# The four weight sums of a seven-product block scheme: written by VectorE instead of GpSimd

## The chip, the cores and the metric

The kernel runs on one core of one Trainium2 chip. The metric is the device time of one execution in microseconds. The engines are TensorE (PE in the profile; PEld is its weight load), VectorE (DVE, `V` in the code), ScalarE (ACT, `S`), GpSimd (POOL, `G`) and SyncE (SP), which issues the DMAs. Each engine works through its own queue in order.

## The reference, cut to what matters

One layer of a diffusion transformer: 2048 latent tokens and 128 prompt tokens of width 1024, differential attention and a short convolution, then a dense feed-forward of hidden width 2816. The change lies in the first half of the feed-forward, the products with `w_ffn_in`:

```python
D_FF = -(-8 * D_MODEL // (3 * 256)) * 256
...
    u = rms_norm(x, g_ffn_pre) * (1.0 + scale_f) + shift_f
    gu = u @ w_ffn_in
    h = jax.nn.silu(gu[..., :D_FF]) * gu[..., D_FF:]
    return x + gate_f * rms_norm(h @ w_ffn_out, g_ffn_post)
```

## The kernel before

The kernel has three long stages: projections and attention, then the feed-forward up products (`gu` and `h`, called the up stage here), then the feed-forward down products (`h @ w_ffn_out`). All numbers are fp32. TensorE multiplies a rounded form (fp32r), so every operand is split in two: `split` makes the rounded high part with a copy on ScalarE (line 81, `CAST` in the trace) and the remainder with a subtraction (line 82), by default on VectorE. Each product is then three matmuls: high by high, high by low and low by high.

The up stage does not multiply the blocks directly. The tokens of a chunk are taken in two halves, and the weights of one block of 128 hidden columns as a 2 by 2 arrangement `a11, a12, a21, a22` (gate and up columns by the two halves of the 1024 inputs), each 128x512. Seven products of combined blocks replace eight. The combinations of the weights are four sums or differences, made by `total` (lines 914 to 917) inside `wi_ops`: `s1 = a21 + a22`, `s2 = s1 - a11`, `s3 = a11 - a21`, `s4 = a12 - s2`. Their buffer `st` has two slots. The seven operands `a11, s1, s2, a12, s3, s4, a22` are split into tiles called `wi`: six of them in three buffers that hold two operands each, the seventh in another pair of buffers. A buffer can be written again when TensorE has done the products that read it.

There are three chunks of tokens (320, 384 and 384 columns wide) and 22 blocks of hidden columns, so 66 units; `wi_ops` runs again for each of them, since the weights are loaded anew for each chunk. A unit has 84 matmuls (7 products, 4 slices of the contraction, 3 matmuls each, lines 954 to 956) into four accumulators `ba` to `bd`. Between products ScalarE copies accumulators (lines 965, 968, 970), VectorE adds (lines 976 `c22` and 979 `u2`, shown as `c` and `u`), and ScalarE, GpSimd (line 982) and VectorE (line 985) form the hidden rows `hid`, which SP stores.

Raw weights come in 512 KB loads, `raw<-in_w_fi`, two for each unit, into the pool `t4` with four slots, one unit ahead. During the first and the second chunk `build_spilled` also prepares the token operands of the following chunk, three times in each: it loads rows into the same `t4` slots (`row`), scales them on GpSimd (line 833), transposes them on TensorE and forms differences on GpSimd (line 857, `td`). Each result is split into `hl`, which has one buffer, and stored to memory (`u2d<-hl`) before the following one may be written. The third chunk has no such work.

The order of the instructions on each engine is not that of the source. A planner orders them when the kernel is compiled, by a simulated run with a table of costs, so it can interleave neighbouring units. Each engine then follows that order and waits where an operand is not ready.

Of the kernel before, what the change touches and what calls it, by code (L numbers as in the profile page):

```python
# [40 lines left out]
def layer(ctx, tc, x_prompt, x_sample, cache_k, cache_v, cond, w_ada, b_ada, gcol,  # L41
# [3 lines left out]
    V, S, G, T = nc.vector, nc.scalar, nc.gpsimd, nc.tensor  # L45
# [33 lines left out]
    def split(h, l, src, eng=None):  # L79

        S.copy(h, src)  # L81
        (eng or V).tensor_tensor(l, src, h.bitcast(F32), op=ALU.subtract)  # L82
# [828 lines left out]
    def wi_ops(raws):  # L911
        a11, a12, a21, a22 = (r[:, i * 512:(i + 1) * 512] for r in raws for i in range(2))

        def total(x, y, op):
            t = sm_.tile([P, 512], F32, tag="st", name="st", bufs=2)
            G.tensor_tensor(t, x, y, op=op)  # L916
            return t

        dst = []
        for k in range(4):  # L920
            if k < 3:
                km = pk.tile([P, NALL], F32R, tag="km", name="wi", bufs=3)
                dst += [(km[:, 1024 * q:1024 * q + 512], km[:, 1024 * q + 512:1024 * q + 1024]) for q in range(2)]
            else:
                q = pk.tile([P, 2, 512], F32R, tag="qt", name="wi", bufs=2)
                dst.append((q[:, 0], q[:, 1]))
        split(*dst[0], a11)
        s1 = total(a21, a22, ALU.add)
        split(*dst[1], s1)
        s2 = total(s1, a11, ALU.subtract)  # L930
        split(*dst[2], s2)
        split(*dst[3], a12)
        s3 = total(a11, a21, ALU.subtract)
        split(*dst[4], s3)
        s4 = total(a12, s2, ALU.subtract)
        split(*dst[5], s4)
        split(*dst[6], a22)
        return dst
# [218 lines left out]
```

## Time and profile before

| what | value |
|---|---|
| time, median of 3 runs | 3038.56 us (3036.72 to 3039.07) |
| profiled execution, time | 3041.68 us |
| profiled execution, span on the core | 3039.9 us |
| TensorE clock granted, mean | 0.987 |
| up stage in the trace | 1520 to 2512 us |

The profile describes one execution, whose own time is 3041.68 us. Engine shares are averages over the three stages. The up stage has three stretches in the trace, one for each chunk: about 1520 to 1840, 1840 to 2190 and 2190 to 2512 us. In a row `wi<-st` names the tile that is written and the tile that is read, `x264` is a count, and `<-` in a wait points to what was waited for.

### The profile page before, as it was taken

To read this page: it belongs to the slowest core of one execution; us is meant where nothing else is said; L and a number is where in the kernel's file an instruction comes from. 1 tells how busy PE (TensorE), PEld (TensorE's weight loads), DVE (VectorE), ACT (ScalarE), POOL (GpSimd) and SP (SyncE) were. 2 spreads that over 40 slices of the span, in tenths; PEclk is the share of its full clock that TensorE was granted. 3 is DMA by queue.
4 is the path that set the end of the run, shared out by engine and by line. 5 is a ranking of instruction groups with operands and counts; after the bars stand their busy time and mean duration, and the time that the engine had idled before them with its cause. 6 is when DMAs were issued, how large, how long until landed. Compare 5 with 4: busy or idle time off the path is not lost.

```text
span 3039.9 us, 47168 instructions
## 1 busy us (share of the span) xinstructions
PE 2902.1 (95%) x16925; PEld 2647.5 (87%) x16925; DVE 1961.1 (65%) x3768; ACT 1466.6 (48%) x2707; POOL 1204.6 (40%) x1106
## 2 busy tenths in 40 slices
PE   6999989999999999999999999999999999999998
PEld 4777789998999998988889989999999998788886
DVE  5998477877888888753367765566555554554443
ACT  5333346665556655554455554445444443434332
POOL 5332135455455454522255654555444440111110
PEclk9999999999999999999999999999999999999999
DMA  8886654454354454457554565445633335766663
GB/s 320 286 306 232 197 177 134 133 168 137 119 178 125 120 165 117 127 182 220 173 159 146 151 196 197 152 152 178 231 102 100 104 103 199 243 218 221 217 218 119
DMA packets 353483, 533.64 MB, mean 176 GB/s; under 512 B 33344, under 2 KB 264928, under 8 KB 351456
## 3 DMA queue, kind: packets, MB, share of 16 engines
q1 hardware_dynamic: 353248, 530.62, 54.2%
q8 instruction: 133, 2.18, 0.3%
q14 instruction: 102, 0.84, 0.1%
HBM read 402.18 MB, written 128.34 MB: 175 GB/s over the span
## 4 chain that ended last, share of the span: by engine, by line
PE 63%; DVE 12%; DMA 10%; issue 8%; POOL 4%; ACT 3%; SPq 0%; DVEq 0%; POOLq 0%; ACTq 0%
PE s L499 7%; PE psg L956 6%; PE psg L954 6%; PE psg L955 6%; PE psy L1086 5%; PE psy L1085 5%; PE psy L1084 5%; PE t L543 3%; DMA u2d<-hl 3%; DVE jv L137 2%; DVE wi L82 2%; PE psx L722 2%; PE psx L723 2%; PE psx L721 2%; PE o L536 2%
## 5 line engine op out<-in xcount | busy, mean ns | idle before, releaser
L954 PE MATMUL psg<-u,wi 128*128 128x384 f32 (+1 forms) x1848 | 607.2, 332 | 26.0 <-ACT wi L81 10.3
L956 PE MATMUL psg<-u,wi 128*128 128x384 f32 (+1 forms) x1848 | 597.1, 329 | 10.0 <-DVE wi L82 10.0
L955 PE MATMUL psg<-u,wi 128*128 128x384 f32 (+1 forms) x1848 | 606.5, 328 | 0.0
L502 DVE TENSOR_SCALAR_CACHE_REDUCE e<-s 128x436 f32<-128x436 f32 (+2 forms) x648 | 373.8, 600 | 85.6 <-PE s L499 68.4
L954 PEld LDWEIGHTS psg<-u,wi 128*128 128x128 f32 x1848 | 349.3, 189 | 36.9 <-ACT wi L81 14.2
L956 PEld LDWEIGHTS psg<-u,wi 128*128 128x128 f32 x1848 | 347.8, 189 | 14.0 <-DVE wi L82 13.7
L499 PE MATMUL s<-km,qt 128*128 128x436 f32 (+1 forms) x1280 | 345.7, 374 | 12.3 <-DVE e L502 8.3
L955 PEld LDWEIGHTS psg<-u,wi 128*128 128x128 f32 x1848 | 350.1, 189 | 0.3
L82 DVE TENSOR_TENSOR wi<-st,wi 128x512 fp32r<-128x512 f32 x264 | 245.2, 932 | 157.7 <-ACT wi L81 154.8
L82 DVE TENSOR_TENSOR wo<-rawo,wo 128x1024 fp32r<-128x1024 f32 x132 | 167.0, 1265 | 252.8 <-ACT wo L81 252.8
L507 ACT ACTIVATE e<-e,nm 128x2176 f32<-128x2176 f32 (+1 forms) x136 | 274.0, 2014 | 78.5 <-DVE nm L506 77.8
L81 ACT CAST wi<-st 128x512 fp32r<-128x512 f32 x264 | 163.2, 619 | 279.2 <-PE psg L956 191.1
L1086 PE MATMUL psy<-wo,hhl 128*128 128x512 f32 x748 | 286.1, 391 | 1.8 <-DVE hhl L82 1.8
L1085 PE MATMUL psy<-wo,hhl 128*128 128x512 f32 x748 | 286.7, 391 | 0.9 <-DVE wo L82 0.9
L1084 PE MATMUL psy<-wo,hhl 128*128 128x512 f32 x748 | 286.3, 391 | 0.0
L81 ACT CAST wo<-rawo 128x1024 fp32r<-128x1024 f32 x132 | 139.1, 1054 | 295.4 <-PE psy L1086 285.2
L82 DVE TENSOR_TENSOR wi<-raw,wi 128x512 fp32r<-128x512 f32 x198 | 233.2, 1194 | 35.6 <-ACT wi L81 29.3
L499 PEld LDWEIGHTS s<-km,qt 128*128 128x128 f32 x1280 | 210.6, 192 | 23.3 <-DVE e L502 14.1
L81 ACT CAST ath<-t 128x512 fp32r<-128x512 f32 (+2 forms) x292 | 157.4, 554 | 114.8 <-PE t L543 112.2
L82 DVE TENSOR_TENSOR atl<-t,ath 128x512 fp32r<-128x512 f32 (+2 forms) x292 | 187.2, 649 | 36.4 <-ACT ath L81 35.6
L1057 POOL TENSOR_TENSOR rr<-rr,mhalf 128x1 f32<-128x1 f32 x17 | 13.1, 779 | 452.7 <-DVE rr L1056 452.7
L916 POOL TENSOR_TENSOR st<-raw,st 128x512 f32<-128x512 f32 x66 | 87.2, 1321 | 252.4 <-DVE wi L82 252.4
(261 smaller groups left out, 6991.5 us busy)
## 6 DMA issues: line engine op xcount, KB each, us to landing
raw<-in_w_fi SPq DMA_DIRECT2D x132, 512.0 KB, 4.2
rawo<-in_w_fo SPq DMA_DIRECT2D x132, 512.0 KB, 3.5
fu<-ud SPq DMA_DIRECT2D x256, 256.0 KB, 4.5
raw<-in_w_ada SPq DMA_DIRECT2D x64, 512.0 KB, 5.9
u2d<-hl SPq DMA_DIRECT2D x42, 512.0 KB, 3.9
u<-u2d SPq DMA_DIRECT2D x14, 1536.0 KB, 10.1
hr<-hid SPq DMA_DIRECT2D x110, 192.0 KB, 3.5
hid<-hid SPq DMA_DIRECT2D x88, 192.0 KB, 3.6
```

The source lines that it names most:

```text
L81: S.copy(h, src)
L82: (eng or V).tensor_tensor(l, src, h.bitcast(F32), op=ALU.subtract)
L499: mm = T.matmul(ps[:, :n], qt[:, s, m, t * P:(t + 1) * P], km[m][:, k0:k0 + n], start=(s == 0), stop=(s == 1))
L502: V.tensor_scalar(et[:, k0:k0 + n], ps[:, :n], SCALE, None, op0=ALU.mult, op1=ALU.max, accum_out=mx[:, ci:ci + 1])
L507: S.activation(et[:, :nk], et[:, :nk], AF.Exp, bias=nm, scale=1.0, accum_out=sm[:, t, m:m + 1])
L543: T.transpose(tp[:, j, t * P:(t + 1) * P], a[t][:, (k0 + j) * P:(k0 + j + 1) * P], ident)
L954: T.matmul(ps, h[:, ks], u[:, 0, kt, :n], start=start and kt == 0, stop=False, skip_group_check=not start)
L955: T.matmul(ps, h[:, ks], u[:, 1, kt, :n], start=False, stop=False, skip_group_check=not start)
L956: T.matmul(ps, l[:, ks], u[:, 0, kt, :n], start=False, stop=kt == 3, skip_group_check=not start)
L1084: T.matmul(banks[i][:, b, :], hh, woh_[:, bs], start=(f == 0), stop=False)
L1085: T.matmul(banks[i][:, b, :], hh, wol_[:, bs], start=False, stop=False)
L1086: T.matmul(banks[i][:, b, :], hl, woh_[:, bs], start=False, stop=(f == NF - 1))
```

## The change

The four sums of each unit are issued to VectorE's queue in place of GpSimd's. Operands, buffers and the rest of the program text are the same.

```diff
         def total(x, y, op):
             t = sm_.tile([P, 512], F32, tag="st", name="st", bufs=2)
-            G.tensor_tensor(t, x, y, op=op)
+            V.tensor_tensor(t, x, y, op=op)
             return t
```

## Rows read from the trace of the kernel before

**Rows 1.** The page: busy time, share of the span and instructions of each engine.
```profile
span 3039.9 us, 47168 instructions
PE 2902.1 (95%) x16925; PEld 2647.5 (87%) x16925; DVE 1961.1 (65%) x3768; ACT 1466.6 (48%) x2707; POOL 1204.6 (40%) x1106
```

**Rows 2.** Windows, one for each chunk: length, then busy time of each engine.
```profile
core 0: us, PE busy (x) PEld busy (x) DVE busy (x) ACT busy (x) POOL busy (x), PEclk, DMA share, GB/s
1520.00:1840.00 320.00, 298.31 (x1938) 288.11 (x1937) 222.78 (x250) 166.21 (x350) 187.04 (x135) 0.98 0.52 161
1840.00:2190.00 350.00, 332.21 (x1877) 323.46 (x1876) 205.70 (x242) 163.00 (x332) 177.89 (x127) 0.99 0.54 175
2190.00:2512.00 322.00, 322.00 (x1858) 321.86 (x1857) 175.20 (x220) 136.35 (x263) 147.42 (x108) 1.00 0.35 118
```

**Rows 3.** Waits of 1520 to 2190: total us, times, longest us.
```profile
POOL st L916 <- DVE wi L82: 142.3, 57, 13.1
...
ACT hl L81 <- DMA u2d<-hl: 70.8, 28, 5.4
ACT wi L81 <- POOL st L916: 60.0, 64, 2.7
DVE hl L82 <- ACT hl L81: 56.8, 26, 5.3
...
POOL st L916 <- DMA raw<-in_w_fi: 31.6, 9, 5.2
...
PEld psg L954 <- ACT wi L81: 14.2, 15, 2.1
...
PEld psg L956 <- DVE wi L82: 13.7, 13, 1.9
PEld psg L954 <- ACT psg L965: 11.5, 12, 2.1
...
ACT wi L81 <- DMA raw<-in_w_fi: 8.1, 8, 2.1
...
PEld psg L954 <- DVE c L976: 5.6, 6, 1.4
```

**Rows 4.** The chain of waits of 1520 to 2190, shares by line.
```profile
by line: DMA u2d<-hl 14.0%; PE psg L956 13.2%; PE psg L954 13.2%; PE psg L955 12.9%; issue 11.3%; DVE wi L82 8.9%; POOL st L916 6.6%; DMA raw<-in_w_fi 4.1%; DVE hl L82 2.5%; DMA row<-x2d 2.2%; ACT wi L81 1.7%; ACT hl L81 1.5%; DMA u<-u2d 1.
```

**Rows 5.** Groups by line on DVE, 1520 to 2512: busy us, mean ns, idle before.
```profile
L82 DVE TENSOR_TENSOR wi<-st,wi 128x512 fp32r<-128x512 f32 x264 | 245.2, 932 | 157.7 <-ACT wi L81 154.8
L82 DVE TENSOR_TENSOR wi<-raw,wi 128x512 fp32r<-128x512 f32 x198 | 233.2, 1194 | 35.6 <-ACT wi L81 29.3 <-PE psx L723 4.7 <-DMA raw<-in_w_fi 1.2
```

**Rows 6.** Groups by line on POOL, 1520 to 2512.
```profile
L916 POOL TENSOR_TENSOR st<-st,raw 128x512 f32<-128x512 f32 x66 | 105.4, 1598 | 25.1 <-issue 13.8 <-POOL st L916 4.8 <-POOL td L857 2.1
L916 POOL TENSOR_TENSOR st<-raw 128x512 f32<-128x512 f32 x66 | 104.9, 1590 | 32.5 <-DMA raw<-in_w_fi 30.9
L916 POOL TENSOR_TENSOR st<-raw,raw 128x512 f32<-128x512 f32 x66 | 95.4, 1446 | 56.1 <-DVE wi L82 55.7
L916 POOL TENSOR_TENSOR st<-raw,st 128x512 f32<-128x512 f32 x66 | 87.2, 1321 | 252.4 <-DVE wi L82 252.4
L982 POOL TENSOR_TENSOR hid<-u,c 128x384 f32<-128x384 f32 (+1 forms) x66 | 70.5, 1068 | 53.3 <-ACT u L980 53.2
```

**Rows 7.** Tile view of `wi`: duration ns min/median/max of the splits.
```profile
L82 DVE TENSOR_TENSOR wi<-st,wi x264: 674/696/1790, 1527.6 to 2500.1; 128x512 fp32r<-128x512 f32 x132
```

**Rows 8.** Timeline of DVE, 1691 us: start us, us.
```profile
1691.16 0.70 DVE L82 TENSOR_TENSOR wi<-st,wi 128x512 fp32r<-128x512 f32 x1 [1.66 <-ACT wi L81]
1691.78 1.76 DVE L82 TENSOR_TENSOR wi<-raw,wi 128x512 fp32r<-128x512 f32 x1
```

**Rows 9.** Timeline of POOL over the same time.
```profile
1691.27 1.72 POOL L916 TENSOR_TENSOR st<-raw 128x512 f32<-128x512 f32 x1
```

**Rows 10.** Groups by line on DVE in the third chunk, 2190 to 2512.
```profile
L82 DVE TENSOR_TENSOR wi<-raw,wi 128x512 fp32r<-128x512 f32 x63 | 77.0, 1247 | 1.9 <-ACT wi L81 1.9
L82 DVE TENSOR_TENSOR wi<-st,wi 128x512 fp32r<-128x512 f32 x86 | 63.8, 742 | 73.1 <-ACT wi L81 73.1
```

## The prediction

> **What bounds the kernel now.** I read the page's busy times first. TensorE is busy for 95% of the span and VectorE for 65% [rows 1], so a change on VectorE counts only where TensorE waits. Next I cut the up stage into windows, one for each chunk [rows 2]. In the third chunk TensorE is busy for 322.00 of 322 us: nothing that the other engines do faster can shorten it, and they can only spoil it. In the first two chunks TensorE is idle for 320 - 298.31 = 21.7 and 350 - 332.21 = 17.8 us, together 39.5 us. That is about the most that the change can win.
>
> Then the waits of the first two chunks [rows 3]. TensorE's weight loads wait 14.2 us for the rounded weights from ScalarE and 13.7 us for the remainders from VectorE, 27.9 us on late weights. They wait 11.5 us for ScalarE's copy of an accumulator and 5.6 us for VectorE's `c22`; these two have other causes. The same view shows where lateness starts: ScalarE stands 28 times, 70.8 us in all, until the one `hl` buffer has been stored, VectorE stands 56.8 us (26 times) for ScalarE's `hl`, and ScalarE waits 60.0 us for GpSimd's sums.
>
> Last the chain of waits over these 670 us [rows 4]. TensorE is on it with 39%, the store of `hl` with 14.0%, VectorE's weight splits with 8.9%, GpSimd's sums with 6.6%. So the sums and splits do lie on the path in places, beside a larger cause that the change leaves alone.
>
> **What goes from GpSimd.** 264 sums take 105.4 + 104.9 + 95.4 + 87.2 = 392.9 us, 1.488 us each [rows 6]. GpSimd keeps line 982 (70.5 us) and the work for the next chunk. Its total in the three windows is 187.04 + 177.89 + 147.42 = 512.3 us [rows 2], so 119 us remain. `td`, `row` and `hid` no longer queue behind sums; since GpSimd is idle for nearly half of the stage before, I count nothing for that. The loads of raw weights can follow sooner when the last sum frees a slot; they are hidden wherever TensorE doesn't wait, and I count nothing there either.
>
> **What comes to VectorE.** A sum reads two 128x512 fp32 tiles and writes a third, as the split of `st` does; that one takes 0.674 us at least, 0.696 in the median and 1.790 at most [rows 7]. These are the bounds for a sum; I take 0.69, as the largest reader beside it on GpSimd is gone. 264 x 0.69 = 182 us.
>
> **What gets cheaper on VectorE.** A split of the same shape took 0.70 us just before a GpSimd sum began, and 1.76 us beside a GpSimd sum of 1.72 us [rows 8, 9]. The 462 weight splits take 245.2 + 233.2 = 478.4 us, a mean of 1.035 [rows 5]. At 0.69 they would take 318.8, so 159.6 us go. VectorE's load thus rises by 182.2 - 159.6 = 22.6 us on 222.78 + 205.70 + 175.20 = 603.7 us [rows 2], from 61% to 63% of 992 us. If the slow part of the splits shrinks only with GpSimd's remaining share (119 of 512, 23%), 37 us more stay and it is 67%. Either way VectorE does not become the bound. In the third chunk 149 splits at 140.8 us [rows 10] fall to 102.8 and 86 sums add 59.3: 175.2 - 38.0 + 59.3 = 196.5 of 322 us, so TensorE stays covered there. If all these sums took 1.79 us, they alone would add 154 us and VectorE would reach 291 us (175.2 - 38.0 + 154), still below 322. I cost the third chunk at zero.
>
> The Trainium skill (Perfetto Trace Analysis, section Optimizing Scalar/DVE Operations) says that moving operations between these two engines might not help, because they share an SBUF read port. The load sum above agrees with it: what the splits gain the sums spend. By the page's rule alone the time would not move, 3038.6 us; this is the second rival.
>
> **What the path gains.** Of the 670 us, the chain puts 6.6% = 44.2 us on sums, 8.9% = 59.6 on splits, 4.1% = 27.5 on raw loads and 1.7% = 11.4 on ScalarE's casts [rows 4], 142.7 us of making weights. With 0.69 for 1.488 the sums become 20.5, with 0.69 for 1.035 the splits 39.7. That cuts 43.6 us, or 31%. I do not book 43.6 us, since most of it is cover for TensorE; I apply the 31% to the 27.9 us that TensorE really stands for weights: -8.5 us. The bounds are zero (every late weight is late because of the `hl` store) and -27.9 (none is).
>
> **Clock.** The granted clock is 0.98 and 0.99 in the two windows and 1.00 in the third [rows 2]. Of the two levels, 2.4 and 1.2 GHz, that means about 12.8 + 7.0 us at the lower, of which half, 9.9 us, is lost. The waits named add up to 27.9 + 11.5 + 5.6 = 45.0; if 8.5 of 45 go, 19% of 9.9 = -1.9 us.
>
> **What the move adds.** A sum now stands in VectorE's queue behind whatever waits there, and other things stand behind it. It waits for raw weights: GpSimd waited for them 31.6 us in 9 waits, ScalarE 8.1 us [rows 3]. On VectorE `c22`, `u2`, `hid` and the splits are queued behind it, and TensorE's accumulators behind those. Bounds: zero if the planner puts the sum where the weights have landed, +31.6 if VectorE stands as GpSimd did. I take a value near the lower end, because ScalarE, which needs the same loads, hardly stood: six waits for `c22` each become longer by half a sum, 6 x 0.69 / 2 = +2.1 us.
>
> **Sum.** -8.5 - 1.9 + 2.1 = -8.3 us. The profiled execution took 3041.7 us (its span 3039.9), so 3033.4 on its scale. It lies 3.1 us above the median of the runs, 3038.56, so the forecast is 3030.3, say 3030 us.
>
> **Rivals.**
> First, the forecast: fewer stalls on late weights, 3022 to 3036, about 3030 us. For it: the chain has both rows that shrink. Against it: the `hl` store is larger than both. Chance 0.42.
>
> Second, no change: the weights are late because ScalarE stands behind the `hl` store, and VectorE spends on sums what it gains on splits. 3033 to 3044, about 3038.6 us. For it: 70.8 us of waits for that store, 14.0% of the chain. Against it: 60.0 us of ScalarE waiting for GpSimd's sums [rows 3]. Chance 0.26.
>
> Third, slower: the sums queue behind VectorE's `hl` split. Before, GpSimd could prepare two sums while VectorE and ScalarE stood; now they come after. The place is the 26 waits of VectorE for `hl`; the price is up to two sums, 1.38 us, before ScalarE has something to cast, 35.9 us if TensorE has no weights in hand. It decides when more than (8.5 + 1.9) / 1.38 = 8 of the 26 lose both sums. At half of them, 17.9 - 10.4 = +7.5 gives 3046 us; at all, +25.5 gives 3064 us. For it: VectorE's queue is in order. Against it: a sum is often ready long before, since GpSimd waited 142.3 us for a slot only. Chance 0.24.
>
> Fourth, much faster: all late weights go, -27.9 us and 27.9 / 45 of the lost clock, -6.1: 3004.6 us. Against it: the store stays. Chance 0.08.
>
> **How the numbers follow.** The point is that of the first case. About 0.2%, 6 us, is what a measurement of this kernel can tell from no change. Faster by more than that: 0.42 + 0.08 = 0.50; within: 0.26; slower: 0.24. The range reaches from 3012, which leaves out most of the fourth case, to 3054, which takes in the third up to some 18 of the 26; about 0.16 lies outside. The first case's own range is 3022 to 3036.
>
> **What the changed profile would show.** Right: line 916 on DVE, 264 at 0.67 to 0.8 us; weight splits at a mean under 0.8; GpSimd down by about 393 us; VectorE's total up by 20 to 60 us; TensorE's waits for weights in the first two chunks at about 19 us, and those chunks shorter by 8 us together; the third unchanged at 320 us. Wrong: TensorE gaps in the third chunk; `hl` waits that now carry sums behind them; waits of line 916 for raw weights with `c22` late behind them; or another order of TensorE's products, since the planner's simulated run sees other costs. The last is the weakest point: it can change every wait that I have read, in either direction, without any row here to size it.

## The result, and the profile after

The kernel after takes 3017.6 us (median of four runs, 3012.83 to 3018.52) against 3037.64 us before (four runs). The ratio is 0.9931, with an interval of 0.9916 to 0.9946: 0.7% faster, about 21 us. The forecast was 3030 us, 8 us faster. The direction held and the range of 3012 to 3054 holds the time. The first case's own range, 3022 to 3036, does not: the gain is some two and a half times the one worked out.

The profiled execution of after is the fastest of its four runs (3012.83 us), and that of before (3041.68) lies above all its timed runs. The two traces therefore differ by 28.9 us, some 8 us more than the kernels do. Sizes read from this pair alone are somewhat too large.

First the page of after, which answers [rows 1].

```profile
span 3010.7 us, 47129 instructions
PE 2892.4 (96%) x16925; PEld 2644.8 (88%) x16925; DVE 2019.8 (67%) x4032; ACT 1464.4 (49%) x2707; POOL 838.4 (28%) x842
```

GpSimd has lost 366 us (393 expected; line 982 alone takes 17 us more, 87.6 for 70.5) and VectorE has gained only 58.7, though 264 instructions came to it. Next the windows of after, cut where the chunks begin, in the columns of [rows 2].

```profile
1523.00:1820.00 297.00, 287.03 (x1896) 279.91 (x1897) 227.22 (x339) 162.17 (x342) 53.59 (x41) 0.99 0.55 169
1820.00:2163.00 343.00, 332.84 (x1899) 326.16 (x1898) 226.64 (x332) 164.46 (x336) 56.33 (x40) 1.00 0.55 179
2163.00:2484.00 321.00, 321.00 (x1854) 321.00 (x1853) 205.59 (x304) 135.27 (x263) 31.09 (x23) 1.00 0.35 117
```

For a fair comparison these are the first two chunks of before, cut in the same way instead of at the round borders of [rows 2].

```profile
1525.00:1837.00 312.00, 290.36 (x1898) 281.33 (x1897) 220.99 (x248) 162.97 (x342) 185.57 (x132) 0.98 0.52 160
1837.00:2190.00 353.00, 335.21 (x1895) 326.46 (x1894) 206.88 (x244) 164.53 (x335) 179.06 (x128) 0.99 0.54 175
```

The gain sits where it was looked for. From first matmul to first matmul (the third to its last) the chunks took 312.2, 353.6 and 320.1 us before, and 297.1, 342.9 and 320.1 after: -15.1, -10.7 and 0. In the first two, TensorE's idle time fell from 21.6 + 17.8 = 39.4 to 10.0 + 10.2 = 20.1 us, which is 19.3 us. The same matmuls also kept it busy for 5.7 us less (290.36 + 335.21 against 287.03 + 332.84), at a granted clock nearer to 1.00.

The groups of after on VectorE over the whole up stage answer [rows 5] and [rows 6].

```profile
L82 DVE TENSOR_TENSOR wi<-st,wi 128x512 fp32r<-128x512 f32 x264 | 194.9, 741 | 106.6 <-ACT wi L81 102.0
L82 DVE TENSOR_TENSOR wi<-raw,wi 128x512 fp32r<-128x512 f32 x198 | 140.1, 722 | 9.9 <-ACT wi L81 9.8
L916 DVE TENSOR_TENSOR st<-raw 128x512 f32<-128x512 f32 x66 | 72.7, 1101 | 12.9 <-DMA raw<-in_w_fi 11.2
L916 DVE TENSOR_TENSOR st<-raw,st 128x512 f32<-128x512 f32 x66 | 55.0, 833 | 2.1
L916 DVE TENSOR_TENSOR st<-raw,raw 128x512 f32<-128x512 f32 x66 | 48.7, 738 | 1.7
L916 DVE TENSOR_TENSOR st<-st,raw 128x512 f32<-128x512 f32 x66 | 45.3, 686 | 1.1
L979 DVE TENSOR_TENSOR u<-psg,p 128x384 f32<-128x384 f32 (+1 forms) x66 | 35.2, 533 | 69.3 <-PE psg L956 69.3
...
L82 DVE TENSOR_TENSOR hl<-td,hl 128x512 fp32r<-128x512 f32 x24 | 16.5, 689 | 19.2 <-ACT hl L81 18.9
```

The weight splits fell from 478.4 to 194.9 + 140.1 = 335.0 us, a mean of 0.725 us against 1.035. The splits of `hl` became quicker too (`hl<-td` 0.689 us). Line 979, which has one operand in TensorE's accumulators, takes 533 ns, and took 531 before. Here are these two groups of before:

```profile
L979 DVE TENSOR_TENSOR u<-psg,p 128x384 f32<-128x384 f32 (+1 forms) x66 | 35.0, 531 | 64.0 <-PE psg L956 64.0
L82 DVE TENSOR_TENSOR hl<-td,hl 128x512 fp32r<-128x512 f32 x24 | 23.6, 983 | 35.0 <-ACT hl L81 35.0
```

So the splits, which read two tiles in SBUF (the memory that holds every tile but the accumulators), became faster, and line 979 did not. The sums cost 72.7 + 55.0 + 48.7 + 45.3 = 221.7 us, 0.840 us each instead of 0.69: their first form, `st<-raw`, stands out with 1.10 us.

Last the waits of after over its first two chunks, which answer [rows 3].

```profile
ACT hl L81 <- DMA u2d<-hl: 54.4, 26, 4.5
...
ACT wi L81 <- DVE st L916: 35.9, 41, 2.3
...
DVE hl L82 <- ACT hl L81: 33.1, 18, 4.7
...
DVE st L916 <- DMA raw<-in_w_fi: 11.2, 6, 2.9
...
PEld psg L954 <- ACT psg L965: 9.5, 12, 2.4
...
PEld psg L954 <- ACT wi L81: 7.1, 11, 1.7
...
PEld psg L956 <- DVE wi L82: 3.1, 4, 0.9
...
PEld psg L954 <- DVE c L976: 1.7, 3, 0.8
```

TensorE now waits 7.1 + 3.1 = 10.2 us for late weights, where it waited 27.9. The waits for `c22` did not grow, they fell from 5.6 to 1.7. VectorE stands 11.2 us for raw weights, where GpSimd stood 31.6.

### The profile page after: what moved, and what is told of

Same layout as the page of the kernel before. It is cut to its first block, busy times and chain, and to the rows that moved or that the text cites. A ratio compares the mean times of both kernels' runs of the same rounds, so it can differ in the third digit from the quotient of the medians.

```text
span 3010.7 us, 47129 instructions
## 1 busy us (share of the span) xinstructions
PE 2892.4 (96%) x16925; PEld 2644.8 (88%) x16925; DVE 2019.8 (67%) x4032; ACT 1464.4 (49%) x2707; POOL 838.4 (28%) x842
## 5 line engine op out<-in xcount | busy, mean ns | idle before, releaser
L507 ACT ACTIVATE e<-e,nm 128x2176 f32<-128x2176 f32 (+1 forms) x136 | 274.0, 2015 | 79.2 <-DVE nm L506 78.3
L82 DVE TENSOR_TENSOR wi<-st,wi 128x512 fp32r<-128x512 f32 x264 | 194.9, 741 | 106.6 <-ACT wi L81 102.0
L982 POOL TENSOR_TENSOR hid<-u,c 128x384 f32<-128x384 f32 (+1 forms) x66 | 87.6, 1328 | 612.3 <-ACT u L980 609.1
L543 PE MATMUL t<-ident,e 128*128 128x128 f32 x1092 | 170.4, 276 | 9.7 <-DVE atl L82 5.5
L536 PE MATMUL o<-atl,vv 128*128 128x256 f32 x548 | 172.4, 315 | 2.5 <-DVE atl L82 1.5
```

The lines of the kernel that those rows point to most:

```text
L507: S.activation(et[:, :nk], et[:, :nk], AF.Exp, bias=nm, scale=1.0, accum_out=sm[:, t, m:m + 1])
L536: T.matmul(o[:, :w], vh, al[:, j, :w], start=False, stop=(k == nkt - 1))
```

## The experiments

The planner set another order of the instructions after the change, so in some kernels every queue of the up stage is pinned to a given order, by dependencies that carry no semaphore. For each instruction `i` in that order:

```diff
...
+        if i.engine in last:
+            tc.add_manual_dep(i, last[i.engine], mybir.DependencyInfo(
+                mybir.DependencyClass.NoSync, mybir.DependencyReason.DATA), reason="order")
+        last[i.engine] = i.name
...
```

### Is it the planner's order?

`e1_v_order_before` has the sums on VectorE and every queue in the order of before. `e2_g_order_after` has them on GpSimd and every queue in the order of after.

> Sums on VectorE as in the changed kernel, but every engine's queue pinned to the order that the planner gave the kernel before (the sums put into VectorE's queue at the place that they had in the planner's overall sequence). Theory A, shorter work (a sum at about 0.7 us for 1.49, splits no longer beside a GpSimd sum): the gain stays, 3016 to 3022 us. Theory B, the planner's other order: the gain goes, 3035 to 3041 us. If both share: about 3028 us.

> Sums on GpSimd as in the kernel before, but every queue pinned to the order of the changed kernel. Theory A, shorter work: no gain, 3035 to 3043 us. Theory B, the planner's other order: 3016 to 3022 us. If both share: about 3028 us.

The first took 3018.03 us against 3040.98, ratio 0.9927 (0.9913 to 0.9941): the whole gain. The second took 3040.36, ratio 1.0000 (0.9990 to 1.0011): none of it. The order is not the cause. In e1 the profiled run (3020.72 us) lies close to its median, so its waits are the better measure of size. Here they are for its first two chunks; lines 1019 and 1021 are lines 954 and 956 of before, and 1030 and 1041 are 965 and 976.

```profile
PEld psg L1019 <- ACT wi L146: 10.9, 12, 3.6
...
PEld psg L1021 <- DVE wi L147: 7.9, 9, 2.3
...
PEld psg L1019 <- ACT psg L1030: 7.1, 9, 2.1
...
PEld psg L1019 <- DVE c L1041: 0.4, 1, 0.4
```

Late weights fell from 27.9 to 18.8 us. ScalarE's copies and `c22` together fell from 17.1 to 7.5.

### Does the third chunk take part?

`e4_third_chunk_only` moves the sums only there.

```diff
-            V.tensor_tensor(t, x, y, op=op)
+            (V if c == 2 else G).tensor_tensor(t, x, y, op=op)
```

> Sums on VectorE in the third chunk only (22 units), on GpSimd in the first two. All theories: no change, 3034 to 3041 us, since TensorE never stands in the third chunk; a rival by which sums in VectorE's queue hold up the accumulators there would give 3045 us or more.

3037.04 us, ratio 0.9988 (0.9977 to 0.9999). The third chunk took 320.1 us, as in both kernels. Nearly nothing is won there, and nothing lost.

### Is it VectorE that gains, or GpSimd that goes quiet?

`e3_shadow` is the kernel after, in its own order, in which GpSimd computes each sum once more into a tile that nobody reads.

```diff
             V.tensor_tensor(t, x, y, op=op)
+            j = sm_.tile([P, 512], F32, tag="sj", name="sj", bufs=2)
+            G.tensor_tensor(j, x, y, op=op)
```

> The changed kernel in its own order, and GpSimd also computes each of the 264 sums from the same operands into a tile that nobody reads. So GpSimd is again busy beside the splits, but no weight waits for its result. Theory C, the gain is that VectorE's splits (and sums) no longer run beside GpSimd: the splits go back to a mean of about 1.0 us and the time to 3030 us or more. Theory D, the gain is the shorter way of the sum itself: 3016 to 3023 us, even with slow splits.

3121.47 us, ratio 1.0263 (1.0248 to 1.0279): 80 us slower than before. Its groups on VectorE and GpSimd show both engines slowed; line 149 is line 82.

```profile
L149 DVE TENSOR_TENSOR wi<-st,wi 128x512 fp32r<-128x512 f32 x264 | 276.1, 1048 | 40.4 <-ACT wi L148 35.8
L149 DVE TENSOR_TENSOR wi<-raw,wi 128x512 fp32r<-128x512 f32 x198 | 235.9, 1206 | 7.5 <-DMA raw<-in_w_fi 4.8 <-ACT wi L148 2.7
```
```profile
L985 POOL TENSOR_TENSOR sj<-raw,raw 128x512 f32<-128x512 f32 x66 | 114.8, 1739 | 0.0
```

The splits are back at 512 us and the four sums on VectorE cost 283.6. VectorE is busy for 313.58 of 356 us in the first chunk, and the third chunk stretches to 329.0 us. While GpSimd goes on reading the same tiles, the move does not pay.

### Contention, or the way through GpSimd?

Contention means here that VectorE's operations take longer because of what GpSimd does beside them; the way through GpSimd is the wait for the sum itself. Three kernels in the order of before take the two apart. All three leave the sums out of the products, as their expectations say.

`e5_sums_unused`: GpSimd computes the sums as before, but the splits read a fixed tile and wait for none of them. `e6_no_sums`: the sums are gone as well.

```diff
+    fixed = sm_.tile([P, 512], F32, name="fixed")
+    V.memset(fixed, 0.02)
...
-        split(*dst[1], s1)
+        split(*dst[1], fixed)
```

`e9_fill`: the splits wait for GpSimd again and read its tile, but GpSimd only fills that tile and reads nothing.

```diff
-            t = sm_.tile([P, 512], F32, tag="st", name="st", bufs=2)
-            G.tensor_tensor(t, x, y, op=op)
-            return t
+            t = sm_.tile([P, 1280], F32, tag="st", name="st", bufs=2)
+            G.memset(t, 0.02)
+            return t[:, :512]
```

> The order of the kernel before, pinned. GpSimd still makes all 264 sums, but nothing reads them except the following sum: the four splits take a fixed tile in place of s1 to s4 (this part of the computation is left out). So nobody waits for a sum, and the splits still run beside GpSimd. Theory C, contention is the cost: splits at about 1.0 us, 3030 to 3040 us. Theory D, the way through GpSimd is the cost: 3014 to 3022 us.

> As the run before, but the sums are left out altogether, on every engine: no wait for a sum and no GpSimd sum beside the splits. The most that can be won from the sums. Theory C and D both: splits at about 0.7 us and 3005 to 3016 us; the step from the run before to this one is the price of contention (C: 15 us or more; D: under 6 us), the step from the changed kernel to this one the price of 182 us of sums on VectorE.

> The order of the kernel before, pinned. In place of each sum GpSimd fills the st tile (made 1280 wide so that it takes about as long as a sum) with a constant, and the splits wait for it and read it as they did the sum; the sums themselves are left out. So the wait for GpSimd stays, but GpSimd reads nothing beside the splits. Theory C, contention is the cost: splits at about 0.7 us and 3004 to 3012 us. Theory D, a share of 10 us for the way through GpSimd: 3012 to 3020 us with splits at 0.7 us. A third, that any GpSimd work beside a split slows it, whether it reads or not: splits at 1.0 us and 3030 us or more.

With the wait gone and GpSimd's reading kept (e5): 3039.6 us, 1.0001 (0.9992 to 1.0010). With both gone (e6): 3004.11 us, 0.9887 (0.9873 to 0.9901). With the wait kept and the reading gone (e9): 3000.11 us, 0.9867 (0.9846 to 0.9888). e6 and e9 came out 1 and 4 us below what was expected of them. The groups on VectorE follow suit, first of e5, then of e6, then of e9; lines 147 and 144 are line 82.

```profile
L147 DVE TENSOR_TENSOR wi<-fixed,wi 128x512 fp32r<-128x512 f32 x264 | 286.2, 1091 | 74.3 <-ACT wi L146 72.9
L147 DVE TENSOR_TENSOR wi<-raw,wi 128x512 fp32r<-128x512 f32 x198 | 242.0, 1238 | 28.5 <-ACT wi L146 20.9 <-DMA raw<-in_w_fi 4.8
```
```profile
L144 DVE TENSOR_TENSOR wi<-fixed,wi 128x512 fp32r<-128x512 f32 x264 | 206.2, 782 | 175.4 <-ACT wi L143 174.0
L144 DVE TENSOR_TENSOR wi<-raw,wi 128x512 fp32r<-128x512 f32 x198 | 144.6, 733 | 48.8 <-ACT wi L143 41.0 <-DMA raw<-in_w_fi 4.5
```
```profile
L147 DVE TENSOR_TENSOR wi<-st,wi 128x512 fp32r<-128x512 f32 x264 | 207.4, 786 | 180.2 <-ACT wi L146 179.5
L147 DVE TENSOR_TENSOR wi<-raw,wi 128x512 fp32r<-128x512 f32 x198 | 145.5, 739 | 48.8 <-ACT wi L146 45.2
```

The splits take 528.2 us beside sums that nobody reads, 352.9 beside fills that everybody waits for, and 350.8 in e6 beside nothing. GpSimd is not idle in e9, as its own groups show:

```profile
L981 POOL MEMSET st<- 128x1280 f32 x264 | 305.1, 1170 | 218.4 <-DVE wi L147 216.6 <-PE psx L788 1.4
```

Two limits of these runs. In e5 the splits suffer more than in before (528 against 478 us), since its sums no longer wait for free slots of `st` and fall beside splits more often; so e5 may hide a gain from the wait that went. An estimate: the splits lose 528 - 351 = 177 us in e5 and 478 - 351 = 128 us in before (351 is e6); if the 35 us between e5 and e6 go with that loss, before's share is 25 us, and up to 10 us could have been the wait. In e9 a fill is shorter than a sum was (1.17 against 1.49 us) and needs no raw weights, so a sum's wait for its loads is not in it. In e5 the sums still hold the slots of the raw weights; ScalarE and VectorE wait for those loads 0.8 + 4.8 = 5.6 us there and 3.0 + 4.5 = 7.5 in e6, so the 35 us between the two are not in these waits. The constant operand is not the cause either, since e5 and e6 both have it.

### The store of `hl`

`e7_before_two_hl` is before, and `e8_after_two_hl` is after, each with two `hl` buffers.

```diff
-            hl = bld.tile([P, 2, 4, P], F32R, tag="hl", name="hl", bufs=1)
+            hl = bld.tile([P, 2, 4, P], F32R, tag="hl", name="hl", bufs=2)
```

> The kernel before with two hl buffers in place of one, so ScalarE and VectorE don't stand for the store of each hl (70.8 us of waits). Theory E, the store is the larger cause of late weights: 3015 to 3028 us. Theory A, the sums and the slowed splits are: 3032 to 3040 us.

> The changed kernel with two hl buffers. Theory E: the rest of the late weights goes too, 3002 to 3012 us. Theory A: little is left for the store, 3013 to 3020 us. Either way it should be at least as fast as the changed kernel.

e7: 3029.51 us, 0.9968 (0.9956 to 0.9981), some 10 us. ScalarE's wait for the store falls from 70.8 to 14.2 us, late weights from 27.9 to 16.1, yet the waits for `c22` rise to 11.5. The time lies between the two ranges that were expected. e8: 3011.16 us, 0.9907 (0.9893 to 0.9922), against 0.9931 without the second buffer. It lies in the range expected if the store matters, but these two intervals overlap, so the further 7 us are likely, not shown. The store, the largest share of the chain in [rows 4], was worth less than half of what the contention was.

### Versions that go on in the same direction

GpSimd still multiplies in line 982. `e12_hid_on_v` moves that too; `e10_two_hl_hid_on_v` has the second `hl` as well; `e11_two_hl_no_gpsimd` adds lines 833 and 857.

```diff
-        G.tensor_tensor(hb, u2_, c22, op=ALU.mult)
+        V.tensor_tensor(hb, u2_, c22, op=ALU.mult)
```

> The changed kernel (one hl buffer) with the product of line 982 on VectorE too. In the changed kernel the splits and sums still take 16 and 40 us more than at 0.69 each, mostly beside line 982. Priced as the earlier runs showed (about 35 us of time for 177 us of slowed splits; about 13.5 us of time for 222 us of sums on VectorE), taking line 982 away wins 56 x 0.2 = 11 us and costs 66 x 0.55 x 0.06 = 2 us: 3007 to 3011 us if before is at 3038. Rival: line 982 costs nothing where it is, 3015 to 3020 us.

> The changed kernel with two hl buffers and also the product of line 982 (66 times, 87.6 us on GpSimd in the changed kernel) on VectorE. Theory C: contention falls further, but VectorE takes 66 times about 0.55 us more; near 3006 to 3013 us, no clear difference to the changed kernel with two hl buffers (3011). Rival: the product's way through GpSimd held up nothing and VectorE's queue now delays accumulators: 3015 us or more.

> As the run before, and the differences and row scalings for the following chunk (lines 833 and 857) on VectorE too: GpSimd has no elementwise work left in the up stage. Theory C: no contention at all, all splits at 0.68 to 0.70 us; VectorE takes 24 x 0.69 and 12 x about 1 us more: 3004 to 3012 us. Rival, VectorE is then too full during the builds: 3015 us or more.

e12 took 3002.62 us, 0.9875 (0.9856 to 0.9895), e10 2995.27 us, 0.9848 (0.9827 to 0.9870), and e11 2994.85 us, 0.9848 (0.9826 to 0.9870). All three are faster than I had priced. So moving line 982 pays, and emptying GpSimd of its last work adds nothing that can be measured, though the splits and the sums of e11 then take 0.69 us in every group. In e12 the sum that stood out is no longer slow in the mean, and line 982 itself takes 0.58 us on VectorE, where it took 1.07 on GpSimd in [rows 6] and 1.33 in after:

```profile
L916 DVE TENSOR_TENSOR st<-raw 128x512 f32<-128x512 f32 x66 | 48.1, 729 | 10.7 <-DMA raw<-in_w_fi 9.8
...
L982 DVE TENSOR_TENSOR hid<-u,c 128x384 f32<-128x384 f32 (+1 forms) x66 | 38.2, 579 | 0.9 <-DMA hid<-hid 0.7
```

That the 15 us of e12 come from the quicker neighbours is argued, not shown: the queues of e12 were not pinned, and its late weights are 12.0 + 2.0 us against the 10.2 of after.

## Why the direction was right and the size was not

**Where the gain lies.** Right. It is in the first two chunks; the third stayed at 320.1 us.

**The load on VectorE.** Nearly right. The splits lost 143.4 us (159.6 expected) and the sums brought 221.7 (182.2 expected), +78.3 together, where the forecast had +22.6. The page shows +58.7, at the upper end of 20 to 60: the `hl` splits lost 10 us, and the page counts time once where instructions overlap, as the two of [rows 8] do. The price of 0.69 us for a sum failed above all for the `st<-raw` form, and line 982 is the largest reader that GpSimd has left. By start and length of each in the trace, 37 of these 66 sums run beside line 982, with a mean of 1.35 us; the other 29 take 0.79. The timeline of after shows one, first VectorE, then GpSimd:

```profile
1635.65 0.69 DVE L916 TENSOR_TENSOR st<-raw,st 128x512 f32<-128x512 f32 x1
1636.38 1.25 DVE L916 TENSOR_TENSOR st<-raw 128x512 f32<-128x512 f32 x1
```
```profile
1635.70 1.38 POOL L982 TENSOR_TENSOR hid<-u,c 128x320 f32<-128x320 f32 x1 [2.36 <-ACT u L980]
```

**The step that failed.** It is the sizing of the path's gain: -8.5 us, as 31% of the 27.9 us of late weights, with the other two waits set aside because "these two have other causes", and +2.1 us for `c22` behind sums. In the queue order of before (e1) the late weights fell by 27.9 - 18.8 = 9.1 us, so by itself that term was of the right size. What was set aside fell as well: copies and `c22` lost 17.1 - 7.5 = 9.6 us where the forecast had them 2.1 longer, and TensorE's busy time fell by 4.2 us, not 1.9. In after's own order the late weights lost 17.7 and the other two 5.9 us, so the shares differ between the two orders. Over the first two chunks, one profiled execution for each kernel, these four lines of waits are, in us:

| kernel | weight splits | late weights | copies, line 965 | `c22` | sum |
|---|---|---|---|---|---|
| before | slow, 478 | 27.9 | 11.5 | 5.6 | 45.0 |
| e2, sums on GpSimd | slow, 475 | 25.1 | 14.6 | 2.1 | 41.8 |
| e5, sums unread | slow, 528 | 29.7 | 8.8 | 3.9 | 42.4 |
| e1, sums on VectorE | quick, 334 | 18.8 | 7.1 | 0.4 | 26.3 |
| after | quick, 335 | 10.2 | 9.5 | 1.7 | 21.4 |
| e6, no sums | quick, 351 | 8.6 | 7.2 | 0.2 | 16.0 |
| e9, fills | quick, 353 | 6.8 | 4.7 | 0 | 11.5 |

Where the splits are slow the sum is above 40 us, whether or not anyone waits for a GpSimd sum; where they are quick it is 12 to 26. So the slow splits stood behind late weights and also behind `c22`, which queues behind them on VectorE: the forecast lengthened those waits by 2.1 us, and in e1 they fell by 5.2. For ScalarE's copies no link is shown: they are 8.8 us with slow splits in e5 and 9.5 with quick ones in after.

**What the 31% stood on.** The chain in [rows 4] put 44.2 us on sums and 59.6 on splits, and I credited both alike. e5 and e9 say, within the limits named above, that the sums' share was worth nothing that these runs can measure and that the slow splits were the price. So it is in part luck that 8.5 us come close to the 9.1 of e1: of the 43.6 us behind the 31%, 44.2 - 20.5 = 23.7 were the sums'. The chain of e5 shows how it misleads: it still puts 6.9% on sums that no product uses.

```profile
by line: PE psg L1021 18.2%; PE psg L1023 18.2%; PE psg L1022 17.7%; issue 11.2%; DMA u2d<-hl 8.3%; DVE wi L147 7.3%; POOL st L983 6.9%; DMA raw<-in_w_fi 2.6%; DVE hl L147 1.5%; ACT wi L146 1.4%; POOL hid L1049 1.1%; PE psg L904 1.1%; ACT h
```

**The account that the runs give.** GpSimd's sums cost the kernel about 35 us (e5 to e6: 3039.6 - 3004.1), for the most part by contention; whether up to 10 of these were a wait in before stays open. Carrying them on VectorE gives back about 12 us (0.9927 of e1 against 0.9887 of e6, the same order, at 3040 us). The net is the 21 to 23 us measured. My two terms for this were -8.5 - 1.9 and +2.1: both too small, by a factor of three and of six.

**The rivals.** No change (0.26) is refuted. The Trainium skill's rule behind it (Perfetto Trace Analysis, Optimizing Scalar/DVE Operations) says that moving work between the two engines might not help. VectorE's busy time over the up stage rose from 602 to 659 us, so the splits did not win back all that the sums cost; so far the rule holds. The time did not follow it, at 0.9931. Slower (0.24) did not come: the waits of VectorE for `hl` fell from 56.8 to 33.1 us, and ScalarE waits 35.9 us for sums where it waited 60.0. Much faster (0.08, 3004.6 us) was too strong for the change, but is about the size that the contention has in e6. The planner's order, called the weakest point, moved nothing (e1, e2).

## What to carry to other kernels

When an operation moves between GpSimd and VectorE, price what it does to its neighbours, not only its own time or its share of the chain: here the neighbours' 143 us of slowed splits decided, and TensorE's waits for `c22` shrank with those for weights. Two runs separate contention from latency: leave the work and let nobody wait for it, and leave the wait and take the reads away. Pin the queues' order before comparing, so that a planner's new order is not taken for the effect.

## What the runs showed of the hardware that I had not expected

A GpSimd operation that only writes did not slow VectorE, though GpSimd was busy with fills for 305 us (393 with sums in before). The timeline of e9 over 6 us shows it, first GpSimd, then VectorE.

```profile
1552.05 1.17 POOL L981 MEMSET st<- 128x1280 f32 x1 [0.33 <-DVE wi L147]
1554.37 1.13 POOL L898 TENSOR_SCALAR row<-row,r2s 128x1024 f32<-128x1024 f32 x1 [1.16 <-DMA row<-x2d]
1555.44 2.28 POOL L981 MEMSET st<- 128x1280 f32 x2
```
```profile
1552.51 0.69 DVE L147 TENSOR_TENSOR wi<-st,wi 128x512 fp32r<-128x512 f32 x1
1554.62 1.41 DVE L147 TENSOR_TENSOR wi<-st,wi 128x512 fp32r<-128x512 f32 x1 [1.43 <-ACT wi L146]
1555.96 0.68 DVE L147 TENSOR_TENSOR wi<-raw,wi 128x512 fp32r<-128x512 f32 x1
```

The split at 1552.51 lies wholly within a fill and takes 0.69 us, as does the one at 1555.96 (0.68). The one between them runs beside the scaling of `row`, which reads SBUF, and takes 1.41 us. Over the whole up stage 97 weight splits lie for at least 0.6 us beside a fill in e9, with a median of 0.70 us; in before 164 lie so beside a sum, with a median of 1.56 us (counted from the start and length of each in the two traces).

The Trainium skill (SBUF — State Buffer, Who interferes with whom) states this: a VectorE instruction with two SBUF inputs contends with a GpSimd instruction that reads SBUF, not with one that only writes it. The traces agree, with 1.56 us beside a sum and 0.70 beside a fill, and with line 979, which reads one operand from TensorE's accumulators and kept its 0.53 us.
